# Recurrent layer of a four-layer network: gate products on unsplit float32 operands, GpSimd's multiplications moved to VectorE, a tile of its own for the recurrence's result, longer lags

## The chip, the cores and the metric

One core of a Trainium2 chip runs the whole network in one launch. The metric is the device time of that core in microseconds. Before the change it was 1740.22 us, the median of three runs (1738.8 to 1741.41).

## The reference

Four layers work on 256 tokens of width 1024 (the first two on a second stream of 256 tokens too). The third layer's first half is the recurrent mixer, and it alone is changed:

```python
def rg_lru(x, w_a, b_a, w_x, b_x, lam):
    xb = x.reshape(bsz, s, N_LRU_BLOCKS, LRU_BLOCK)
    r = jax.nn.sigmoid(jnp.einsum("bsnd,nde->bsne", xb, w_a).reshape(bsz, s, w) + b_a)
    i = jax.nn.sigmoid(jnp.einsum("bsnd,nde->bsne", xb, w_x).reshape(bsz, s, w) + b_x)
    log_a = (-LRU_C * r.astype(jnp.float32)) * jax.nn.softplus(-lam.astype(jnp.float32))
    a = jnp.exp(log_a)
    mult = jnp.sqrt(-jnp.expm1(2.0 * log_a))
    u = mult * (i * x).astype(jnp.float32)
    ...  # h[t] = a[t] * h[t-1] + u[t]

def recurrent_mixer(...):
    gate, xr = jnp.split(hn @ w_in, 2, axis=-1)
    xr = causal_depthwise_conv(xr, conv_w, conv_b)
    y = rg_lru(xr, gate_a_w, gate_a_b, gate_x_w, gate_x_b, lam)
    return (y * jax.nn.gelu(gate)) @ w_out
```

The width of the recurrence is 1408, which is 11 tiles of 128 channels. The two gate products are block-diagonal with 16 blocks of 88 channels, so a tile of gates needs two or three tiles of xr: 31 pairs of tiles in all, and 62 products of 128 x 128 weights with 128 x 256 activations.

## The kernel before

Activations stand with channels on partitions and the 256 tokens along the free axis. Every large product is made in three matmuls of a reduced-precision float32 type (fp32r): weights and activations are each split into a rounded high part and a rest, and `mm3` (L338 to L340) adds high x high, high x low and low x high into one PSUM bank. `load_w` (L309 to L315) fetches a weight piece into the buffer `st`, rounds it on ScalarE (`wh`, L311) and subtracts on VectorE (`wl`, L315). There are 6 buffers of `st` and 6 of the pair `wh`, `wl`.

`lru_layer` (L1336) runs over tiles m. Per tile:

- `up(m)` makes tile m of xr: 24 matmuls into a bank called `up`; `leave` (L506, L508) takes it out of PSUM on VectorE into `ldu`, `full` (L512) adds a bias on ScalarE, and `sink_x` applies the convolution, one instruction on ScalarE (L1347) and three on VectorE (L1350), into `xv`. It then splits `xv` into `xh` (ScalarE, L1351) and `xl` (GpSimd, L1352), which the gate products read.
- `gates(m)` loads the gate weights, makes 12 or 18 matmuls into the bank `gt` (L1374), and works out a, the input's factor and the recurrence: tanh, tanh, exp, tanh on ScalarE (L1379 to L1382), then on VectorE the start value and two Newton steps of an inverse square root (L1384 to L1389, a square on ScalarE in each, L1387). GpSimd multiplies twice (L1391, L1393), and a scan on VectorE (L1394) writes the result over `xv`. The eight intermediate rows stand in two buffers `w1`, `w2` of a ring of 4 (tag `lw`), so two tiles of gates fit.
- `sink_g(g)` takes a tile of the other half of the input projection (again 24 matmuls into a bank `up`), applies gelu on ScalarE and VectorE (L1356 to L1359), multiplies by the recurrence's result on GpSimd (L1360) and splits into `yh`, `yl` (L1362, L1363).
- `acc.step(k)` adds the product of y tile k and its output weights to four banks `da` (24 matmuls).

The program before the loop makes xr tiles 0 to 5. In iteration m the order is `up(m + 6)`, `gates(m)`, `sink_g(m - 2)`, `acc.step(m - 5)`; the constants are `LRU_UP` and `LRU_LAGS`. TensorE keeps this written order. On the other engines a scheduler sets the order within their queues when the program is built. Four PSUM banks are shared by `up` and `gt`; the other four are `da`.

Of the kernel before, what the change touches and what calls it, by code (L numbers as in the profile page):

```python
# [10 lines left out]
F32 = mybir.dt.float32  # L11
F32R = mybir.dt.float32r
I32 = mybir.dt.int32
AF = mybir.ActivationFunctionType
ALU = mybir.AluOpType
AX = mybir.AxisListType

P = 128
KD = 8
T = 256  # L20
# [43 lines left out]
NEWTON = [(-1.407904506, 1.681913909), (-1.0, 1.50000036)]  # L64
# [38 lines left out]
EV = ("SSV", "SV", "SVVS")  # L103
TAIL_PRIO = 300
ACC_BUFS = 3
LRU_LAGS = (2, 5, 2)
LRU_UP = 6
PS_FF = (4, 0)
LRU_BUFS = (9, 8, 6)
LAG_FFN = (4, 2)  # L110
LAG_MLP = (6, 2)
RSTD_AT = (4, 7)
# [61 lines left out]
def tile_kernel(ctx: ExitStack, tc: tile.TileContext, I, out, taps=None):  # L174
    nc = tc.nc
    V, S, G, TE = nc.vector, nc.scalar, nc.gpsimd, nc.tensor
# [17 lines left out]
    wbufs = [0, 0]  # L194
    prio = [PRIO0]
# [10 lines left out]
    def tl(name, shape, dt=F32, tag=None, bufs=1, pool="g"):  # L206
        return pools[pool].tile([P] + list(shape), dt, name=name, tag=tag or name, bufs=bufs)

    def lt(name, shape, dt=F32):
        return tl(name, shape, dt, "l", 6)  # L210
# [7 lines left out]
    def bank(name, shape=(512,)):  # L218
        return pools["ps"].tile([P] + list(shape), F32, name=name, tag="b", bufs=psum["b"])
# [17 lines left out]
    def f(ap):  # L237
        return ap.bitcast(F32)
# [12 lines left out]
    def col(name, i=0, n=None):  # L251
        o, w = COLS[name]
        return cols[:, o + i:o + (w if n is None else i + n)]
# [52 lines left out]
    def load_w(src, n=1024, raw=False):  # L306
        with tc.high_priority(offset=prio[0]):
            st = tl("st", [1024], F32, "st", wbufs[0], "w")
            nc.sync.dma_start(st[:, :n], src)  # L309
            hi, lo = [tl("w" + x, [1024], F32R, "w" + x, wbufs[1], "w") for x in "hl"]  # L310
            S.copy(hi[:, :n], st[:, :n])  # L311
            eng = G if pool_next.pop(0) == "G" else V
            if not pool_next:
                pool_next.append("V")
            eng.tensor_tensor(lo[:, :n], st[:, :n], f(hi[:, :n]), ALU.subtract)  # L315
        return (hi, lo, st) if raw else (hi, lo)
# [20 lines left out]
    def mm3(ps, wh, wl, ah, al, first, last, **kw):  # L337
        TE.matmul(ps, lhsT=wh, rhs=ah, start=first, stop=False, **kw)  # L338
        TE.matmul(ps, lhsT=wh, rhs=al, start=False, stop=False, **kw)  # L339
        TE.matmul(ps, lhsT=wl, rhs=ah, start=False, stop=last, **kw)  # L340
# [970 lines left out]
    def lru_softplus():  # L1311


        lam = col("lam")
        n = LRU_K
        t = [st_(f"sp{j}", [n]) for j in range(6)]
        V.tensor_scalar(t[0], lam, -1.0, None, ALU.mult)
        V.tensor_tensor(t[0], t[0], lam, ALU.min)
        S.activation(t[1], t[0], AF.Exp)
        V.tensor_scalar(t[2], t[1], 2.0, None, ALU.add)  # L1320
        V.reciprocal(t[2], t[2])
        V.tensor_tensor(t[2], t[2], t[1], ALU.mult)
        V.tensor_tensor(t[3], t[2], t[2], ALU.mult)
        V.memset(t[4], 1.0 / 17.0)
        for d in (15.0, 13.0, 11.0, 9.0, 7.0, 5.0, 3.0, 1.0):
            V.tensor_tensor(t[4], t[4], t[3], ALU.mult)
            V.tensor_scalar(t[4], t[4], 1.0 / d, None, ALU.add)
        V.scalar_tensor_tensor(t[4], t[4], 2.0, t[2], ALU.mult, ALU.mult)
        V.tensor_scalar(t[5], lam, -1.0, 0.0, ALU.mult, ALU.max)
        V.tensor_tensor(t[4], t[4], t[5], ALU.add)  # L1330
        sp4 = tl("sp4", [2, n])
        V.tensor_scalar(sp4[:, 0, :], t[4], -4.0, None, ALU.mult)
        V.tensor_scalar(sp4[:, 1, :], t[4], 4.0, None, ALU.mult)
        return sp4

    def lru_layer(x, ahead, mod, nxt):  # L1336
        sp4 = lru_softplus()
        hgb = tl("hgb", [22])
        o = COLS["lga"][0]
        V.tensor_scalar(hgb, cols[:, o:o + 22], 0.5, None, ALU.mult)  # L1340
        xs, ys = {}, {}
        lcw = col("lcw")

        def sink_x(m, ps):
            c, (xh, xl) = xs[m] = (tl("xv", [T], F32, "xv", LRU_BUFS[0], "f"),
                                   [tl("x" + y, [T], F32R, "x" + y, LRU_BUFS[1], "f") for y in "hl"])
            S.activation(c, ps, AF.Identity, scale=lcw[:, 33 + m:34 + m], bias=col("lcb", m, 1))  # L1347
            for d in range(1, 4):
                w = lcw[:, (3 - d) * 11 + m:(3 - d) * 11 + m + 1]
                V.scalar_tensor_tensor(c[:, d:], ps[:, :T - d], w, c[:, d:], ALU.mult, ALU.add)  # L1350
            S.copy(xh, c)  # L1351
            G.tensor_tensor(xl, c, f(xh), ALU.subtract)  # L1352

        def sink_g(m, ps):
            sq = lt("lsq", [T])
            S.activation(sq, ps, AF.Square)  # L1356
            V.scalar_tensor_tensor(sq, sq, GELU_IN, ps, ALU.add, ALU.mult)
            S.activation(sq, sq, AF.Tanh, scale=GELU_SC)
            V.scalar_tensor_tensor(sq, sq, 1.0, ps, ALU.add, ALU.mult)  # L1359
            G.tensor_tensor(sq, sq, xs[m][0], ALU.mult)  # L1360
            yh, yl = ys[m] = [tl("y" + y, [T], F32R, "y" + y, LRU_BUFS[2], "f") for y in "hl"]
            S.activation(yh, sq, AF.Copy, scale=0.5)  # L1362
            V.scalar_tensor_tensor(yl, sq, 0.5, f(yh), ALU.mult, ALU.subtract)  # L1363

        def gates(m):
            ks = [k for (mm, k) in GATE_PAIRS if mm == m]
            j0 = [j for j, (mm, k) in enumerate(GATE_PAIRS) if mm == m][0]
            n = len(ks)
            wh, wl = load_w(I["gates"][:, j0:j0 + n].rearrange("p j x c -> p (j x c)"), n * 2 * P)
            b2 = bank("gt", [2, T])  # L1370
            for y in range(2):
                for j, k in enumerate(ks):
                    w = slice((2 * j + y) * P, (2 * j + y + 1) * P)
                    mm3(b2[:, y], wh[:, w], wl[:, w], *xs[k][1], j == 0, j == n - 1)  # L1374
            w1 = tl("w1", [4, T], F32, "lw", 4, "f")
            tr, ti, tau, pv_ = (w1[:, j, :] for j in range(4))
            w2 = tl("w2", [4, T], F32, "lw", 4, "f")
            y, b, u, a = (w2[:, j, :] for j in range(4))
            S.activation(tr, b2[:, 0], AF.Tanh, scale=0.5, bias=hgb[:, m:m + 1])  # L1379
            S.activation(ti, b2[:, 1], AF.Tanh, scale=0.5, bias=hgb[:, 11 + m:12 + m])  # L1380
            S.activation(a, tr, AF.Exp, scale=sp4[:, 0, m:m + 1], bias=sp4[:, 0, m:m + 1])
            S.activation(tau, tr, AF.Tanh, scale=sp4[:, 1, m:m + 1], bias=sp4[:, 1, m:m + 1])  # L1382

            V.scalar_tensor_tensor(pv_, tau, 1.0, tau, ALU.add, ALU.mult)  # L1384
            V.tensor_scalar(y.bitcast(I32), pv_.bitcast(I32), -0.5, RSQRT_SEED, ALU.mult, ALU.add)
            for (c1, c0) in NEWTON:
                S.activation(b, y, AF.Square)  # L1387
                V.scalar_tensor_tensor(b, b, c1, pv_, ALU.mult, ALU.mult)
                V.scalar_tensor_tensor(y, b, c0, y, ALU.add, ALU.mult)  # L1389
            xm = xs[m][0]  # L1390
            G.tensor_tensor(y, y, tau, ALU.mult)  # L1391
            V.scalar_tensor_tensor(u, ti, 1.0, xm, ALU.add, ALU.mult)
            G.tensor_tensor(u, u, y, ALU.mult)  # L1393
            V.tensor_tensor_scan(xm, a, u, 0.0, ALU.mult, ALU.add)  # L1394

        def up(m):
            sink_x(m, ahead.full(ahead.out(load_w(I["lru_in"][1, m]))))

        ws = [load_w(I["lru_in"][1, j]) for j in range(4)]
        with tc.high_priority(offset=LEAD_PRIO):  # L1400
            for j, u in enumerate(ahead.lead(ws)):
                sink_x(j, ahead.full(u))
        for m in range(4, LRU_UP):
            up(m)
        acc = DownAcc(LRU_K, LRU_LAGS[2])
        sink = resid_sink(x, mod[:, 16:24], nxt)
        for m in range(LRU_K + LRU_LAGS[1]):
            k = m - LRU_LAGS[1]
            if m + LRU_UP < LRU_K:
                up(m + LRU_UP)  # L1410
            if m < LRU_K:
                gates(m)
            if 0 <= m - LRU_LAGS[0] < LRU_K:
                g = m - LRU_LAGS[0]
                sink_g(g, ahead.full(ahead.out(load_w(I["lru_in"][0, g]))))
            if k >= 0:
                acc.step(k, I["lru_out"][k], ys[k], sink)
        tap("xl", x)
# [185 lines left out]
    hs = [hl(f"h0{s}", "d") for s in range(2)]  # L1604
# [132 lines left out]
    hs = []  # L1737
# [44 lines left out]
    x, mod = res[0], mods[0]  # L1782
# [193 lines left out]
```

## Time and profile before

| | |
|---|---|
| median of three runs | 1740.22 us |
| the profiled execution | 1737.93 us |
| its span, first to last instruction | 1736.2 us |
| TensorE busy | 1625.7 us (94%) |
| VectorE busy | 1367.9 us (79%) |
| ScalarE busy | 916.7 us (53%) |
| GpSimd busy | 139.8 us (8%) |

In the profile PE is TensorE's matmul, PEld its weight load, DVE VectorE, ACT ScalarE, POOL GpSimd and SP the queue that issues the loads. Times within the span are microseconds from its start. The recurrent layer stands from about 1056 to 1214 us. A busy share over the whole span says little of one layer, so the rows below are cut to the layer's stretch.

### The profile page before, as it was taken

What the parts mean: (1) busy time and instruction counts of PE and PEld (TensorE: products, weight loads), DVE (VectorE), ACT (ScalarE), POOL (GpSimd) and SP (SyncE); (2) the same over time, 40 slices, a digit from 0 to 9 for tenths busy, and PEclk for the clock granted to TensorE, in tenths of its full rate; (3) what the DMA queues carried; (4) which work ended last, traced back from release to release, by engine and by line L of the source; (5) the groups of instructions that cost most, each with busy time, mean ns of one, the idle gap of its engine ahead of it and who ended that gap; (6) DMA issues with size and microseconds to landing.
All of it is one profiled execution on the core that took longest, in us unless ns stands there. A gap on an engine that the chain in (4) does not pass through costs nothing.

```text
span 1736.2 us, 28828 instructions
## 1 busy us (share of the span) xinstructions
PE 1625.7 (94%) x10858; PEld 1404.7 (81%) x10858; DVE 1367.9 (79%) x2799; ACT 916.7 (53%) x1617; POOL 139.8 (8%) x199
## 2 busy tenths in 40 slices
PE   6998989899999998888999999886999999899999
PEld 3784559788888887764899999886999977499999
DVE  5768757589999967778689887987989988569554
ACT  3437654343242434546577666775655554656553
POOL 1110220000000000101000001532000001300000
PEclk9999999999999999999999999998999999999999
DMA  8306536335768633236655553445889843578552
GB/s 309 135 25 225 175 119 205 115 121 186 271 222 303 234 106 104 85 109 207 216 185 183 183 186 127 131 149 183 284 316 345 340 152 128 207 255 288 186 184 72
DMA packets 90714, 327.91 MB, mean 189 GB/s; under 512 B 10064, under 2 KB 10192, under 8 KB 90064
## 3 DMA queue, kind: packets, MB, share of 16 engines
q1 hardware_dynamic: 90288, 323.99, 54.6%
q0 software_dynamic: 288, 2.10, 0.3%
q8 instruction: 85, 1.39, 0.3%
q14 instruction: 53, 0.43, 0.1%
HBM read 325.00 MB, written 1.05 MB: 188 GB/s over the span
## 4 chain that ended last, share of the span: by engine, by line
PE 58%; issue 15%; DVE 9%; POOL 2%; DMA 2%; ACT 2%; POOLq 0%; DVEq 0%; ACTq 0%
PE up L338 8%; PE up L339 8%; PE up L340 7%; PE da L339 4%; PE da L338 4%; PE da L340 4%; DVE wl L315 3%; PE dn L338 2%; PE dn L340 2%; PE dn L339 2%; PE dt L603 2%; PE dt L601 2%; PE dt L602 2%; DMA gst<-in_ada_dram 2%; PE gv L353 1%
## 5 line engine op out<-in xcount | busy, mean ns | idle before, releaser
L311 ACT CAST wh<-st 128x1024 fp32r<-128x1024 f32 (+3 forms) x392 | 400.5, 1030 | 363.6 <-PE up L339 145.2
L315 DVE TENSOR_TENSOR wl<-st,wh 128x1024 fp32r<-128x1024 f32 (+3 forms) x392 | 470.8, 1205 | 95.8 <-ACT wh L311 94.9
L338 PE MATMUL up<-xgh,wh 128*128 128x258 f32 x912 | 259.9, 285 | 5.7 <-DVE ldu L508 3.3
L339 PE MATMUL up<-xgl,wh 128*128 128x258 f32 x912 | 259.8, 285 | 0.0
L340 PE MATMUL up<-xgh,wl 128*128 128x258 f32 x912 | 258.7, 284 | 1.0 <-DVE wl L315 0.9
L338 PEld LDWEIGHTS up<-xgh,wh 128*128 128x128 f32 x912 | 173.4, 190 | 6.6 <-issue 2.2
L340 PEld LDWEIGHTS up<-xgh,wl 128*128 128x128 f32 x912 | 174.6, 191 | 1.4 <-DVE wl L315 1.4
L339 PEld LDWEIGHTS up<-xgl,wh 128*128 128x128 f32 x912 | 174.0, 191 | 0.0
L386 DVE CUSTOM_DVE_ANT_0 gst<-gst,crow,cols 128x1024 f32<-128x1024 f32 x120 | 153.4, 1283 | 14.3 <-DMA gst<-in_kvada_dram 6.7
L338 PE MATMUL up<-h2h,wh 128*128 128x512 f32 (+1 forms) x384 | 143.8, 375 | 5.3 <-ACT h2h L448 5.1
L340 PE MATMUL up<-h2h,wl 128*128 128x512 f32 (+1 forms) x384 | 143.5, 374 | 0.5 <-DVE wl L315 0.5
L338 PE MATMUL da<-g2h,wh 128*128 128x256 f32 x512 | 143.9, 281 | 0.0
L340 PE MATMUL da<-g2h,wl 128*128 128x256 f32 x512 | 143.8, 281 | 0.0
L339 PE MATMUL da<-g2l,wh 128*128 128x256 f32 x512 | 143.7, 281 | 0.0
L339 PE MATMUL up<-h2l,wh 128*128 128x512 f32 (+1 forms) x384 | 143.3, 373 | 0.3 <-DVE h2l L449 0.3
L339 PEld LDWEIGHTS da<-g2l,wh 128*128 128x128 f32 x512 | 96.5, 188 | 0.0
L340 PEld LDWEIGHTS da<-g2h,wl 128*128 128x128 f32 x512 | 96.4, 188 | 0.0
L338 PEld LDWEIGHTS da<-g2h,wh 128*128 128x128 f32 x512 | 96.4, 188 | 0.0
L353 PE MATMUL gv<-gst,cst 128*32 128x512 f32 x352 | 68.7, 658 | 22.5 <-DMA gst<-in_w_ada_dram 15.5
L338 PEld LDWEIGHTS up<-h2h,wh 128*128 128x128 f32 x384 | 73.1, 190 | 18.5 <-ACT h2h L448 5.5
L340 PEld LDWEIGHTS up<-h2h,wl 128*128 128x128 f32 x384 | 73.0, 190 | 13.6 <-DVE wl L315 1.0
L339 PEld LDWEIGHTS up<-h2l,wh 128*128 128x128 f32 x384 | 73.1, 190 | 12.9 <-DVE h2l L449 0.5
(498 smaller groups left out, 3920.8 us busy)
## 6 DMA issues: line engine op xcount, KB each, us to landing
st<-in_mlp_dram SPq DMA_DIRECT2D x128, 512.0 KB, 4.6
gst<-in_w_ada_dram SPq DMA_DIRECT2D x96, 512.0 KB, 4.4
st<-in_w_up_dram SPq DMA_DIRECT2D x88, 512.0 KB, 4.3
gst<-in_ada_dram SPq DMA_DIRECT2D x40, 512.0 KB, 4.2
st<-in_w_in_dram SPq DMA_DIRECT2D x32, 512.0 KB, 3.6
gst<-in_ada21t_dram SPq DMA_DIRECT2D x32, 512.0 KB, 6.4
st<-in_w_down_dram SPq DMA_DIRECT2D x25, 512.0 KB, 3.8
gst<-in_ada20t_dram SPq DMA_DIRECT2D x24, 512.0 KB, 4.6
```

The source lines that it names most:

```text
L311: S.copy(hi[:, :n], st[:, :n])
L315: eng.tensor_tensor(lo[:, :n], st[:, :n], f(hi[:, :n]), ALU.subtract)
L338: TE.matmul(ps, lhsT=wh, rhs=ah, start=first, stop=False, **kw)
L339: TE.matmul(ps, lhsT=wh, rhs=al, start=False, stop=False, **kw)
L340: TE.matmul(ps, lhsT=wl, rhs=ah, start=False, stop=last, **kw)
L353: TE.matmul(ps[32 * t:32 * t + 32, :], lhsT=cst[:, 2 * q + i, :], rhs=st[:, i * 512:i * 512 + 512], start=(q < 2), stop=(q >= 2), tile_pos ...
L386: V.tensor_tensor_reduce(o, st, r, 0.5, bias[:, b:b + 1], ALU.mult, ALU.add, dest[:, v, b:b + 1])
L601: TE.matmul(o, lhsT=hh[:, k, js], rhs=wh[:, wsl], start=(k == 0), stop=False)
L602: TE.matmul(o, lhsT=hh[:, k, js], rhs=wl[:, wsl], start=False, stop=False)
L603: TE.matmul(o, lhsT=hlo[:, k, js], rhs=wh[:, wsl], start=False, stop=(k == KD - 1))
```

## The change

`gates` no longer splits its operands: it loads the weights into `st` and makes one plain float32 matmul per pair from `st` and `xv`. `xh` and `xl` go. The three multiplications of GpSimd go to VectorE, where the factor's second Newton step is applied to the product itself instead of to the root. The scan writes a tile `hv` of its own. The lags become 3 for `sink_g` and 6 for `acc.step`.

```diff
-LRU_LAGS = (2, 5, 2)
+LRU_LAGS = (3, 6, 2)
-LRU_BUFS = (9, 8, 6)
+LRU_BUFS = (9, 5, 6)
...
         def sink_x(m, ps):
-            c, (xh, xl) = xs[m] = (tl("xv", [T], F32, "xv", LRU_BUFS[0], "f"),
-                                   [tl("x" + y, [T], F32R, "x" + y, LRU_BUFS[1], "f") for y in "hl"])
+            c = xs[m] = tl("xv", [T], F32, "xv", LRU_BUFS[0], "f")
...
-            S.copy(xh, c)
-            G.tensor_tensor(xl, c, f(xh), ALU.subtract)
...
             S.activation(sq, sq, AF.Tanh, scale=GELU_SC)
+            V.tensor_tensor(ps, ps, hs.pop(m), ALU.mult)
             V.scalar_tensor_tensor(sq, sq, 1.0, ps, ALU.add, ALU.mult)
-            G.tensor_tensor(sq, sq, xs[m][0], ALU.mult)
...
-            wh, wl = load_w(I["gates"][:, j0:j0 + n].rearrange("p j x c -> p (j x c)"), n * 2 * P)
+            with tc.high_priority(offset=prio[0]):
+                st = tl("st", [1024], F32, "st", wbufs[0], "w")
+                nc.sync.dma_start(st[:, :n * 2 * P], I["gates"][:, j0:j0 + n].rearrange("p j x c -> p (j x c)"))
...
-                    w = slice((2 * j + y) * P, (2 * j + y + 1) * P)
-                    mm3(b2[:, y], wh[:, w], wl[:, w], *xs[k][1], j == 0, j == n - 1)
+                    TE.matmul(b2[:, y], lhsT=st[:, (2 * j + y) * P:(2 * j + y + 1) * P], rhs=xs[k], start=(j == 0),
+                              stop=(j == n - 1))
...
-            for (c1, c0) in NEWTON:
-                S.activation(b, y, AF.Square)
-                V.scalar_tensor_tensor(b, b, c1, pv_, ALU.mult, ALU.mult)
-                V.scalar_tensor_tensor(y, b, c0, y, ALU.add, ALU.mult)
-            xm = xs[m][0]
-            G.tensor_tensor(y, y, tau, ALU.mult)
-            V.scalar_tensor_tensor(u, ti, 1.0, xm, ALU.add, ALU.mult)
-            G.tensor_tensor(u, u, y, ALU.mult)
-            V.tensor_tensor_scan(xm, a, u, 0.0, ALU.mult, ALU.add)
+            (c1, c0), (d1, d0) = NEWTON
+            S.activation(b, y, AF.Square)
+            V.scalar_tensor_tensor(b, b, c1, pv_, ALU.mult, ALU.mult)
+            V.scalar_tensor_tensor(y, b, c0, y, ALU.add, ALU.mult)
+
+            V.scalar_tensor_tensor(u, ti, 1.0, xs[m], ALU.add, ALU.mult)
+            V.tensor_tensor(u, u, tau, ALU.mult)
+            S.activation(b, y, AF.Square)
+            V.tensor_tensor(u, u, y, ALU.mult)
+            V.scalar_tensor_tensor(b, b, d1, pv_, ALU.mult, ALU.mult)
+            V.scalar_tensor_tensor(u, b, d0, u, ALU.add, ALU.mult)
+            h = hs[m] = tl("hv", [T], F32, "hv", LRU_BUFS[1], "f")
+            V.tensor_tensor_scan(h, a, u, 0.0, ALU.mult, ALU.add)
```

The scheduler also reorders the queues. On GpSimd, the stretch of the loop from the third tile on, the change against before (`w_` with a number is a tile's `w1` or `w2`, `lsq` is gelu's):

```order
-L1352 TENSOR_TENSOR xl<-xv,xh 128x256
-L1391 TENSOR_TENSOR w_11540<-w_11540,w_11539 128x256
-L1393 TENSOR_TENSOR w_11540<-w_11540 128x256
-L1360 TENSOR_TENSOR lsq<-lsq,xv 128x256
-L1352 TENSOR_TENSOR xl<-xv,xh 128x256
-L1391 TENSOR_TENSOR w_11674<-w_11674,w_11673 128x256
-L1393 TENSOR_TENSOR w_11674<-w_11674 128x256
-L1360 TENSOR_TENSOR lsq<-lsq,xv 128x256
```

Nothing takes their place: GpSimd has no instruction left in the layer.

On VectorE before, the end of the fourth tile of gates (`w_11674`) and what stands around it, the split of the next gate weights (768 columns) among it:

```order
L315 TENSOR_TENSOR wl<-st,wh 128x1024
L1388 SCALAR_TENSOR_TENSOR w_11674<-w_11674,w_11673 128x256
L506 COPY ldc<-up 128x1
L508 TENSOR_TENSOR ldu<-up,rb 128x256
L1389 SCALAR_TENSOR_TENSOR w_11674<-w_11674 128x256
L1357 SCALAR_TENSOR_TENSOR lsq<-lsq,ldu 128x256
L315 TENSOR_TENSOR wl<-st,wh 128x768
L1394 SCALAR_TENSOR_TENSOR xv<-w_11674 128x256
L1359 SCALAR_TENSOR_TENSOR lsq<-lsq,ldu 128x256
```

The row that writes `xv` is the scan, and between L1389 and it GpSimd's two multiplications run.

On VectorE now, the same part of a tile's work two tiles later (`w_11720`, line numbers of the changed kernel; `hv` is written by the scan):

```order
L1388 SCALAR_TENSOR_TENSOR w_11720<-w_11720,w_11719 128x256
L1392 TENSOR_TENSOR w_11720<-w_11720,w_11719 128x256
L1389 SCALAR_TENSOR_TENSOR w_11720<-w_11720 128x256
L506 COPY ldc<-up 128x1
L508 TENSOR_TENSOR ldu<-up,rb 128x256
L1394 TENSOR_TENSOR w_11720<-w_11720 128x256
L1395 SCALAR_TENSOR_TENSOR w_11720<-w_11720,w_11719 128x256
L1384 SCALAR_TENSOR_TENSOR w_11793<-w_11793 128x256
L1396 SCALAR_TENSOR_TENSOR w_11720<-w_11720 128x256
L1354 SCALAR_TENSOR_TENSOR lsq<-lsq,ldu 128x256
L1398 SCALAR_TENSOR_TENSOR hv<-w_11720 128x256
L1356 TENSOR_TENSOR ldu<-ldu,hv 128x256
```

The multiplications L1392, L1394 and L1356 are new on this engine, no split of gate weights is left, and the scan follows its own engine's row L1396.

## Rows read from the trace of the kernel before

**Rows 1.** Busy time by engine over the whole span (share, instructions)

```profile
PE 1625.7 (94%) x10858; PEld 1404.7 (81%) x10858; DVE 1367.9 (79%) x2799; ACT 916.7 (53%) x1617; POOL 139.8 (8%) x199
```

**Rows 2.** Stretches: us, busy of PE, PEld, DVE, ACT, POOL; clock, DMA share, GB/s

```profile
1069.00:1206.00 137.00, 111.44 (x840) 106.75 (x838) 116.65 (x237) 95.47 (x186) 53.82 (x44) 0.94 0.49 154
1069.00:1121.00 52.00, 43.83 (x349) 42.11 (x348) 46.77 (x98) 41.90 (x83) 26.13 (x17) 1.00 0.44 131
1121.00:1150.00 29.00, 26.21 (x186) 26.01 (x185) 24.81 (x53) 20.45 (x42) 10.63 (x10) 0.83 0.46 142
1150.00:1180.00 30.00, 27.68 (x224) 26.64 (x224) 25.64 (x51) 21.55 (x41) 9.80 (x9) 1.00 0.51 162
1180.00:1206.00 26.00, 13.72 (x88) 11.99 (x86) 19.43 (x38) 11.58 (x23) 7.25 (x8) 0.87 0.61 204
```

**Rows 3.** PE's waits, 1069 to 1206: who for whom; us in total, times, longest

```profile
PE da L338 <- ACT yh L1362: 9.2, 4, 5.7
PE gt L340 <- DVE wl L315: 3.4, 2, 2.8
PE up L338 <- DVE ldu L508: 3.3, 3, 2.0
PE gt L339 <- POOL xl L1352: 2.0, 2, 1.0
PE da L339 <- DVE yl L1363: 2.0, 3, 0.9
PE da L340 <- DVE wl L315: 1.6, 2, 1.1
PE gt L338 <- ACT w L1380: 1.6, 2, 1.2
```

**Rows 4.** Groups on POOL, 1069 to 1206: busy, mean ns, idle before

```profile
L1352 POOL TENSOR_TENSOR xl<-xv,xh 128x256 fp32r<-128x256 f32 x11 | 23.5, 2148 | 256.2 <-ACT xh L1351 256.2
L1391 POOL TENSOR_TENSOR w<-w,w 128x256 f32<-128x256 f32 x11 | 13.4, 1215 | 36.0 <-DVE w L1389 20.1 <-ACT lsq L1358 15.9
```

**Rows 5.** Groups on DVE, 1069 to 1206, same columns

```profile
L315 DVE TENSOR_TENSOR wl<-st,wh 128x768 fp32r<-128x768 f32 x9 | 9.6, 1066 | 0.0
L1394 DVE TENSOR_TENSOR_SCAN xv<-w 128x256 f32<-128x256 f32 x11 | 9.2, 832 | 14.2 <-POOL w L1393 14.2
L1392 DVE SCALAR_TENSOR_TENSOR w<-w,xv 128x256 f32<-128x256 f32 x11 | 6.7, 610 | 0.0
L315 DVE TENSOR_TENSOR wl<-st,wh 128x512 fp32r<-128x512 f32 x2 | 1.4, 680 | 0.0
```

**Rows 6.** PE in order of time, recurrent layer's start: us of start, us, what

```profile
1069.12 0.29 PE L339 MATMUL up<-xgl,wh 128*128 128x258 f32 x1
1069.24 0.29 PE L340 MATMUL up<-xgh,wl 128*128 128x258 f32 x1
```

**Rows 7.** PE in order of time, attention: float32 products with 64 columns

```profile
209.81 1.95 PE L708 MATMUL opb<-pt,Vt 128*64 128x256 f32 x16
211.69 0.66 PE L689 MATMUL tr<-kc,zqb 128*128 128x128 f32 x4
```

**Rows 8.** Single matmuls' durations by tile: ns least/median/most

```profile
L708 PE MATMUL opb<-pt,Vt x160: 379/379/687, 209.8 to 839.0; 128*64 128x256 f32 x160
L339 PE MATMUL gt<-xl,wh x62: 276/281/415, 1078.9 to 1167.6; 128*128 128x256 f32 x62
```

**Rows 9.** PE in order of time, keys' projection: products of 512 columns

```profile
1470.42 0.40 PE L601 MATMUL dt<-wh,kvh 128*128 128x512 f32 x1
1470.66 0.39 PE L602 MATMUL dt<-wl,kvh 128*128 128x512 f32 x1
```

**Rows 10.** DVE in order of time, between two of POOL's instructions

```profile
1142.46 0.41 DVE L1357 SCALAR_TENSOR_TENSOR lsq<-lsq,ldu 128x256 f32<-128x256 f32 x1
1142.79 0.41 DVE L1389 SCALAR_TENSOR_TENSOR w<-w 128x256 f32<-128x256 f32 x1
```

**Rows 11.** Chain that ended last, one tile's first tanh and its scan

```profile
1081.81 0.47 ACT w L1379
1098.64 0.69 DVE xv L1394
```

**Rows 12.** DMA issues: KB each, median us to landing

```profile
st<-in_lru_in_dram SPq DMA_DIRECT2D x22, 512.0 KB, 4.3
```

**Rows 13.** Row sums of a float32 matrix, PE in order of time

```profile
1061.67 1.40 PE L416 MATMUL nps<-ones,acc 128*128 128x2 f32 x12
1062.92 0.36 PE L338 MATMUL da<-xgh,wh 128*128 128x258 f32 x1
```

More of the change, by code (lines that the diff above doesn't have):

```diff
@@ L1340, in lru_layer @@
         V.tensor_scalar(hgb, cols[:, o:o + 22], 0.5, None, ALU.mult)
-        xs, ys = {}, {}
+        xs, hs, ys = {}, {}, {}
         lcw = col("lcw")
         def sink_x(m, ps):
-            c, (xh, xl) = xs[m] = (tl("xv", [T], F32, "xv", LRU_BUFS[0], "f"),
-                                   [tl("x" + y, [T], F32R, "x" + y, LRU_BUFS[1], "f") for y in "hl"])
+            c = xs[m] = tl("xv", [T], F32, "xv", LRU_BUFS[0], "f")
             S.activation(c, ps, AF.Identity, scale=lcw[:, 33 + m:34 + m], bias=col("lcb", m, 1))
```

## The prediction

> **What bounds the kernel now.** I read first the busy time by engine, then the recurrent layer's stretch cut into pieces, then TensorE's waits in it, then the groups on GpSimd and VectorE that stand behind them. Over the whole span TensorE is 94% busy [rows 1], so little is to be had elsewhere. From 1069 us (the layer's lead-in of four tiles is done) to 1206 us (its last output products), TensorE is busy in 111.4 of 137.0 us, and its granted clock averages 0.94 [rows 2]. So 25.6 us are idle, and part of the rest runs at half speed.
>
> The pieces of the stretch [rows 2] differ. From 1069 to 1121 TensorE idles 8.2 us, from 1121 to 1180 5.1 us, from 1180 to 1206 12.3 us. The clock is 0.83 from 1121 to 1150 and 0.87 in the last piece. Between levels of 1.2 and 2.4 GHz, a mean of 0.83 says that 34% of 29 us, 9.9 us, ran at the lower level, which lost half of that, 4.9 us; likewise 26% of the last 26 us lost 3.4 us. Both pieces come behind or hold waits of TensorE.
>
> TensorE's waits [rows 3] name four causes. It waits for `xl`, GpSimd's rest of xr (2.0 us); for gate weights that VectorE splits late (3.4); for banks that ScalarE's tanh or VectorE's `ldu` has not emptied (1.6 and 3.3); and, most of all, for `yh` and `yl` at the end (9.2 and 2.0), with 1.6 for output weights. Behind these stands GpSimd: 11 rests of 2148 ns on the mean, and a first multiplication of 1215 ns [rows 4]. VectorE, busy 116.65 of 137 us [rows 2], idles 14.2 us before its 11 scans, until GpSimd's second multiplication is done [rows 5]. It is an in-order queue, so each such idle delays the weight splits and bank readings behind it.
>
> **The change part by part.**
>
> *Gate products.* 186 fp32r matmuls go. Two in a row start 0.12 us apart [rows 6], so they fill 22.3 us. 62 float32 matmuls come. The trace writes two records for each such matmul: for the row sums the program has 6 (three partial sums, two token halves), the trace 12 [rows 13]. So 124 records are to be priced, and no row has one with 128 x 128 weights and 256 columns. The nearest is attention's, with 64 columns of weights: it lasts 379 ns, against 281 ns for an fp32r one [rows 8]. An fp32r matmul of 512 columns lasts 0.40 us and is followed after 0.24 us [rows 9]. I take 0.24, since the record lasts about as long: 124 x 0.24 = 29.8 us, that is **+7.5 us**. Below, attention's 16 records take 1.88 us [rows 7], 0.1175 each: 14.6 us, or -7.7 us; but their weights fill half the array, and two may run side by side. Above, a weight load that nothing hides adds what a record of two columns takes, 1.25 us / 12 = 0.104 us [rows 13]: 124 x 0.344 = 42.7 us, or +20.4 us. The Trainium skill (FP8 and Floating Point Precision, TensorE Precision Notes) says that true FP32 takes four passes through the array, which speaks against the change: four passes in place of three would be an estimated 29.8 us and +7.5, where attention's row taken as it stands would give -7.7; no run here shows a full-width one.
>
> *GpSimd.* All 53.8 us of its work in the stretch [rows 2] go. This counts only through who waited: the 2.0 us for `xl`, the 1.6 us of banks held by a tanh that could not start before GpSimd had read its buffers, and VectorE's 14.2 us.
>
> *VectorE.* 11 splits of gate weights go, 9.6 + 1.4 = 11.0 us busy [rows 5]. Three instructions per tile come, 33 in all. Undisturbed, such instructions start 0.33 us apart [rows 10]: 10.9 us. So its work stays level, but two disturbances leave: the scans' waits, and the slowing beside GpSimd (L1392 takes 610 ns on the mean, the scan 832 [rows 5], where undisturbed ones take about 410 [rows 10] and 690 [rows 11]; 11 x 0.34 = 3.7 us for these two alone). VectorE's 116.65 us become about 111, in a stretch that I expect to last 116: it stays almost as full as TensorE, so I don't let all waits go.
>
> *ScalarE.* It loses the rounding of gate weights and `xh`, 22 instructions. At 95.5 of 137 us [rows 2] it isn't the bound; I count nothing. Were it the bound, its tanh would hold the banks, as in the rivals.
>
> *Loads.* The gate weights now stay in one of the six buffers `st` until their products have run; the load that reuses it waits so long on the SP queue, and those behind it too. A load lands after 4.3 us [rows 12], and the split takes some 2 us more. Six loads stand for two iterations or more, at least 2 x 5.8 us of TensorE's work (24 x 0.12 + 12 x 0.24). That hides it: 0 us; uncovered it would cost up to 6 us at a tile.
>
> *Lags.* The last gates get two more weight blocks (`sink_g` of a tile and one `acc.step`, 24 x 0.12 = 2.9 us each) of TensorE's work between them and the products that need them, 5.8 us. This covers the longest wait of the end, 5.7 us [rows 3]. No work is added.
>
> *The sum.* From 1069 to 1121 I let 6.5 of 8.2 us go (`xl`, tanh, most of the late `ldu`). From 1121 to 1180 4.1 of 5.1 (the gate weights' 3.4 and part of what is late behind them), with 4.4 of the 4.9 us of slow clock. From 1180 on 10.3 of 12.3, with 3.0 of 3.4. Together -28.3 us; with +7.5, **-20.8 us**. What stays late next is VectorE's queue, with weight splits and `ldu` in the iterations that hold all parts. The profiled execution took 1737.93 us (a span of 1736.2 and 1.7 around it) and lies 2.3 us below the median of 1740.22. So 1737.93 - 20.8 = 1717.1, and for a median **1719 us**.
>
> **The rivals.**
>
> *A, only the named causes go.* VectorE's queue paces the layer as before, with hops to ScalarE where those to GpSimd were. Then `xl` 2.0, gate weights 3.4, tanh 1.6 and half of the slow clock (4.2) go: -11.2 + 7.5 = -3.7, about 1736 us. For it speaks VectorE's 85% share; against it, that its own waits name GpSimd [rows 5].
>
> *B, dear products.* Every weight load is exposed: -28.3 + 20.4 = -7.9, 1732 us. Against it: loads run beside matmuls (PEld and PE are both busy over 100 of 137 us [rows 2]).
>
> *C, nothing stays late.* All 25.6 us and 8.3 us of slow clock go: -33.9 + 7.5 = -26.4, 1714 us; with the low price of the products -41.6, 1699 us. Against it: VectorE's 111 us of work hardly fit below 112 us.
>
> *D, slower.* VectorE gets no relief: its queue has 22 instructions more (33 come, 11 go), its idle 20.35 us stays because each tile's factor still goes to ScalarE for two squares, and each instruction that comes takes 0.41 us: 116.65 - 11.0 + 13.5 + 20.35 = 139.5, +2.5 us, and the products' +7.5 fall where TensorE has no slack: +10 us, 1750 us. It decides the time once VectorE's work and waits exceed 137 us. Against it: 14.2 of the 20.35 us end with GpSimd. The Trainium skill (VectorE: DVE Perf Modes, Rules for kernel authors) says to keep the count of chained VectorE instructions low, and the change raises it; by that rule alone this rival would be the forecast, and no run yet shows it.
>
> **How the numbers follow.** The forecast (a gain of 12 to 28 us) gets 0.67, A 0.12, B 0.07, C 0.08, D 0.06. The range from 1709 to 1732 holds the forecast, B and most of C; it leaves out D, A and C's low end, about 0.2. A measurement of this kernel tells some 0.2%, 3.5 us, from no change. Faster by more: 0.67 + 0.07 + 0.08 and 0.07 of A, 0.89. Within: the rest of A, 0.05. Slower: D, 0.06.
>
> **What would show it.** Right: records of `gt` about 380 ns long, 124 of them, some 0.24 us apart; no GpSimd work in the layer; the scan following VectorE's own rows without idle time; TensorE idle under 8 us in the stretch; the clock near 1.00 throughout; the wait for `yh` under 2 us. Wrong: `gt` records further than 0.3 us apart (B); TensorE idle as before with waits for `ldu` and ScalarE's tanh (A, D); waits for `st` loads. A difference outside the layer would contradict me too.

## The result, and the profile after

The changed kernel takes 1709.87 us (median of four runs, 1708.99 to 1712.81); the kernel before took 1740.63 us in the four runs beside it. The ratio is 0.9824, 95% interval 0.9811 to 0.9838: faster by 1.8%, inside the range and at its low end, 9 us below the forecast of 1719. The profiled execution took 1710.57 us with a span of 1708.8 us, against 1737.93 and 1736.2. One run of the kernel before, beside number 12 below, took 8177.62 us and is left out of the ratio there.

Busy time by engine over the whole span, first line of the page (before: [rows 1]):

```profile
PE 1617.7 (95%) x10796; PEld 1398.4 (82%) x10796; DVE 1360.1 (80%) x2821; ACT 905.1 (53%) x1595; POOL 86.5 (5%) x155
```

TensorE lost 62 instructions: 186 matmuls went and 124 records came. VectorE gained 22, as counted. To compare the layer as a whole I cut both traces from the first product of its lead-in to the first product of the next layer's (columns as in [rows 2]). The kernel before:

```profile
1055.80:1212.99 157.19, 131.55 (x993) 126.69 (x993) 129.81 (x273) 103.62 (x205) 53.82 (x44) 0.93 0.47 150
```

The kernel after, the layer, and then the same pieces as in [rows 2]:

```profile
1055.46:1185.93 130.47, 124.68 (x930) 120.09 (x931) 122.86 (x296) 92.61 (x184) 0.00 (x0) 1.00 0.52 168
...
1069.00:1121.00 52.00, 52.00 (x370) 49.87 (x369) 51.15 (x126) 39.94 (x80) 0.00 (x0) 1.00 0.52 161
1121.00:1150.00 29.00, 29.00 (x212) 27.91 (x211) 28.61 (x70) 22.56 (x44) 0.00 (x0) 1.00 0.56 180
1150.00:1180.00 30.00, 25.21 (x201) 24.01 (x201) 28.61 (x63) 20.76 (x40) 0.00 (x0) 1.00 0.65 215
1180.00:1206.00 26.00, 23.96 (x199) 23.61 (x198) 24.43 (x52) 15.61 (x30) 0.00 (x0) 1.00 0.78 257
```

The layer went from 157.2 to 130.5 us. That is 26.7 of the 27.4 us by which the spans differ, so the gain is the layer's. In the first two pieces TensorE has no idle time at all, the clock is 1.00 everywhere, and the last piece belongs for the most part to the next layer (from 1185.93). The third column of busy times says what comes next: VectorE is busy in 122.9 of the 130.5 us, nearly as full as TensorE (124.7).

TensorE's waits in the layer, same columns as [rows 3]; of the causes there, `xl`, the tanh, `ldu` and the late weight splits are gone:

```profile
PE da L338 <- ACT yh L1359: 3.8, 2, 2.0
PE da L338 <- DVE xres L526: 1.0, 1, 1.0
PE da L339 <- DVE yl L1360: 0.9, 2, 0.6
```

The gate products by tile (ns least/median/most), and in order of time one tile's and what follows it:

```profile
L1373 PE MATMUL gt<-xv,st x124: 377/379/379, 1077.3 to 1146.9; 128*128 128x256 f32 x124
```

```profile
1081.93 2.75 PE L1373 MATMUL gt<-xv,st 128*128 128x256 f32 x12
1084.34 0.47 PE L338 MATMUL up<-xgh,wh 128*128 128x258 f32 x1
```

Twelve records take 1084.34 - 1081.93 = 2.41 us, 0.20 each, although each lasts 379 ns: the next starts when half of it is over. All 124 fill about 24.9 us.

VectorE's groups in the layer (columns as in [rows 5]): the scan has no idle time before it and takes 680 ns where it took 832:

```profile
L315 DVE TENSOR_TENSOR wl<-st,wh 128x1024 fp32r<-128x1024 f32 x33 | 39.9, 1214 | 0.3 <-ACT wh L311 0.3
L1398 DVE TENSOR_TENSOR_SCAN hv<-w 128x256 f32<-128x256 f32 x11 | 7.5, 680 | 0.0
```

Where TensorE still idles: in order of time, its last waits of the layer (idle time before in brackets).

```profile
1169.76 0.27 PE L340 MATMUL da<-yh,wl 128*128 128x256 f32 x1
1172.00 0.39 PE L338 MATMUL da<-yh,wh 128*128 128x256 f32 x1 [1.96 <-ACT yh L1359]
...
1179.00 0.38 PE L338 MATMUL da<-yh,wh 128*128 128x256 f32 x1 [1.80 <-ACT yh L1359]
```

And VectorE in the same time, gelu's steps (`lsq`, `ldu`) towards that `yh`:

```profile
1166.55 2.34 DVE L315 TENSOR_TENSOR wl<-st,wh 128x1024 fp32r<-128x1024 f32 x2
1168.82 0.41 DVE L1354 SCALAR_TENSOR_TENSOR lsq<-lsq,ldu 128x256 f32<-128x256 f32 x1
1169.15 1.21 DVE L315 TENSOR_TENSOR wl<-st,wh 128x1024 fp32r<-128x1024 f32 x1
1170.29 0.41 DVE L1356 TENSOR_TENSOR ldu<-ldu,hv 128x256 f32<-128x256 f32 x1
1170.62 0.14 DVE L506 COPY ldc<-up 128x1 f32<-128x1 f32 x1
1170.69 0.41 DVE L508 TENSOR_TENSOR ldu<-up,rb 128x256 f32<-128x256 f32 x1
1171.02 0.41 DVE L1357 SCALAR_TENSOR_TENSOR lsq<-lsq,ldu 128x256 f32<-128x256 f32 x1
```

Each starts before the one ahead has wholly ended, none waits for another engine, and weight splits stand between the steps: so I read the tile as late because VectorE's queue is full. The row names ScalarE (`yh`), but ScalarE only had to wait for L1357.

### The profile page after: what moved, and what is told of

It is laid out like the page before. It is cut to its first block, busy times and chain, and to the rows that moved or that the text cites. A ratio compares the mean times of both kernels' runs of the same rounds, so it can differ in the third digit from the quotient of the medians.

```text
span 1708.8 us, 28624 instructions
## 1 busy us (share of the span) xinstructions
PE 1617.7 (95%) x10796; PEld 1398.4 (82%) x10796; DVE 1360.1 (80%) x2821; ACT 905.1 (53%) x1595; POOL 86.5 (5%) x155
## 4 chain that ended last, share of the span: by engine, by line
PE 72%; DVE 9%; DMA 3%; ACT 2%; issue 2%; POOL 0%; SPq 0%; DVEq 0%; ACTq 0%; POOLq 0%
PE up L338 10%; PE up L339 10%; PE up L340 10%; PE da L338 6%; PE da L339 6%; PE da L340 6%; DVE wl L315 2%; PE dn L338 2%; PE dn L340 2%; PE dn L339 2%; PE dt L601 2%; PE dt L603 2%; PE dt L602 2%; DMA gst<-in_ada_dram 2%; PE gv L353 1%
## 5 line engine op out<-in xcount | busy, mean ns | idle before, releaser
L311 ACT CAST wh<-st 128x1024 fp32r<-128x1024 f32 (+2 forms) x381 | 392.2, 1037 | 359.3 <-PE up L339 137.2
L315 DVE TENSOR_TENSOR wl<-st,wh 128x1024 fp32r<-128x1024 f32 (+2 forms) x381 | 458.4, 1207 | 93.4 <-ACT wh L311 92.0
```

## The experiments

All ratios are to the kernel before, in the same batch, with 95% intervals. The executions begin the layer up to some 7 us earlier or later (1050 to 1057 us here, behind parts that are the same in all), and what follows it takes 523 to 529 us, so I compare its length too, cut as above, one execution of each kernel. TensorE's idle time in the layer is its length less TensorE's busy time; the same work takes more busy time where the clock is lower.

| kernel | ratio | layer, us | TensorE busy | VectorE busy | clock |
|---|---|---|---|---|---|
| before | 1 | 157.2 | 131.6 | 129.8 | 0.93 |
| after | 0.9824 | 130.5 | 124.7 | 122.9 | 1.00 |
| 1 products alone | 0.9917 | 143.2 | 131.5 | 118.5 | 0.94 |
| 2 multiplications alone | 0.9947 | 147.0 | 126.1 | 134.1 | 0.97 |
| 3 lags alone | 0.9989 | 158.2 | 130.6 | 130.8 | 0.96 |
| 4 after, old lags | 0.9848 | 130.7 | 125.9 | 122.9 | 0.99 |
| 5 after, 11 more multiplications | 0.9872 | 135.8 | 129.2 | 127.0 | 0.96 |
| 6 after, half the gate products | 0.985 | 137.3 | 120.6 | 123.4 | 0.94 |
| 7 after, gelu first at the end | 0.9835 | 132.1 | 126.3 | 122.9 | 0.99 |
| 8 after, float32 output, tiles 7 to 10 | 0.9862 | 133.4 | 128.2 | 120.7 | 0.97 |
| 9 after, float32 output, tiles 0 to 5 | 0.9829 | 129.9 | 127.6 | 116.2 | 1.00 |
| 10 after, float32 output, tiles 0 to 2 | 0.9839 | 128.8 | 125.6 | 119.8 | 1.00 |
| 11 after, float32 output, all tiles | 0.9838 | 129.7 | 129.7 | 109.3 | 1.00 |
| 12 numbers 11 and 6 together | 0.9784 | 122.5 | 117.8 | 107.8 | 1.00 |

### 1 to 4: which part gives the gain

Three theories share the change out: the gain comes from the products (P), from the multiplications that leave GpSimd, so that VectorE's queue no longer waits (V), or from the lags at the layer's end (L).

**1. Products alone.** Before, with the products of the change and the scan's own tile; GpSimd multiplies as before, lags 2 and 5.

```diff
-            S.copy(xh, c)
-            G.tensor_tensor(xl, c, f(xh), ALU.subtract)
...
-                    mm3(b2[:, y], wh[:, w], wl[:, w], *xs[k][1], j == 0, j == n - 1)
+                    TE.matmul(b2[:, y], lhsT=st[:, (2 * j + y) * P:(2 * j + y + 1) * P], rhs=xs[k], start=(j == 0),
+                              stop=(j == n - 1))
...
-            V.tensor_tensor_scan(xm, a, u, 0.0, ALU.mult, ALU.add)
+            V.tensor_tensor_scan(h, a, u, 0.0, ALU.mult, ALU.add)
```

> The kernel before with the unsplit gate products and the result's own tile alone; GpSimd keeps its three multiplications per tile, the lags stay 2 and 5. Theory V (VectorE's queue sets the layer's pace, and its idle time before the scans, until GpSimd has multiplied, is the main loss): those 14 us of idle time stay for the most part, 11 us of weight splits leave VectorE; about 12 us faster than before (1728). Theory P (what was late were the split operands of the gate products): most of the change's 27 to 31 us, 20 us or more (1720 or less). Theory L (the lags): under 8 us.

Measured: 1723.36 us, 0.9917 (0.9896 to 0.9938), some 14 us: between what V and P foresaw, and nearer V. The layer is 14.0 us shorter. VectorE's busy time falls by 11.3 us, the splits; its waits for GpSimd stay (waits of VectorE, 1069 to 1206 us):

```profile
DVE hv L1395 <- POOL w L1393: 13.5, 9, 2.1
```

TensorE's idle time falls by 14.0 us. Its granted clock is still 0.94, and it waits 4.6 us for `yh` and 4.7 for `yl`.

**2. Multiplications alone.** Before, with GpSimd's three multiplications on VectorE and the second Newton step on the product; products split, scan in place, lags 2 and 5.

```diff
-            G.tensor_tensor(y, y, tau, ALU.mult)
...
-            G.tensor_tensor(u, u, y, ALU.mult)
...
+            V.tensor_tensor(u, u, tau, ALU.mult)
+            S.activation(b, y, AF.Square)
+            V.tensor_tensor(u, u, y, ALU.mult)
...
```

> The kernel before with the three multiplications per tile moved from GpSimd to VectorE (and the second Newton step applied to the product) alone; gate products split as before, with GpSimd making xl, old lags. Theory V: the scans' 14 us of idle time go, 11 us of work come to a queue that also keeps the 11 us of splits: about 8 us faster (1732), and VectorE without idle time. Theory P: within 4 us of before. Theory L: the same.

Measured: 1728.6 us, 0.9947 (0.9928 to 0.9966), which V foresaw and P did not; the layer is 10.2 us shorter. VectorE has more work than any other run (134.1 us), and from 1150 to 1180 us no gap at all; TensorE still waits 7.3 us for `yh` (before 9.2, [rows 3]). Its idle time falls by 4.7 us, and its busy time by 5.5 with the same work, which is the clock. Window and waits of this kernel:

```profile
1150.00:1180.00 30.00, 28.70 (x236) 28.25 (x237) 30.00 (x70) 22.66 (x42) 0.00 (x0) 1.00 0.62 189
```

```profile
PE da L338 <- ACT yh L1362: 7.3, 3, 3.5
PE up L338 <- DVE ldu L508: 4.2, 3, 2.0
PE up L340 <- DVE wl L315: 3.9, 3, 1.9
```

**3 and 4. Lags.** Before with lags 3 and 6 (and a tenth `xv`, since the scan still writes there), and the changed kernel with 2 and 5.

```diff
-LRU_LAGS = (2, 5, 2)
+LRU_LAGS = (3, 6, 2)
```

> The kernel before with the lags 3 and 6 alone (and 10 buffers of xv, which the longer lag needs). Theory L: 10 us or more faster (1730 or less), since the 9 to 13 us that TensorE waits for yh and yl at the layer's end go. Theories V and P: VectorE's queue is as late as before, so 5 us at most (1735 or more).

> The changed kernel with the old lags 2 and 5. Theory L: it loses 10 us or more against the changed kernel (1720 or more). Theories V and P: VectorE is still full, so what the lags cover at the end is a few us; 2 to 6 us are lost (1712 to 1716).

Measured: 1735.8 us, 0.9989 (0.9976 to 1.0002), and 1710.99 us, 0.9848 (0.9824 to 0.9872), with layers of 158.2 and 130.7 us. The lags are worth nothing that can be measured, in either kernel; L falls, and so do the 2 to 6 us that V and P foresaw as lost in number 4. In number 3 the wait for `yh` does shrink, from 9.2 to 6.9 us, but the waits for `yl` (2.0 to 4.6) and tanh (2.5 to 4.3) grow by more.

The two parts that count give 14.0 + 10.2 = 24.2 us apart and 26.7 together. What they share is VectorE's queue: its busy time and its wait for GpSimd before the scan are 129.8 + 14.2 = 144.0 us before, 132.0 in number 1, 134.1 in number 2, 122.9 after, which is 12.0, 9.9 and 21.1 us less where the layer is 14.0, 10.2 and 26.7 us shorter. That this queue is the cause fits these sums, and number 5 tests it; number 1 takes away the splits of the gate products' operands and VectorE's work on them at once, and does not part the two.

### 5 to 7: what paces the layer now

Theory Q: VectorE's queue still does.

**5. Eleven more multiplications**, one per tile of gates, by ones.

```diff
             V.tensor_tensor(u, u, tau, ALU.mult)
+            V.tensor_tensor(u, u, wz, ALU.mult)
```

> The changed kernel with one multiplication by one more per tile on VectorE, in the chain before the scan: 11 x 0.335 = 3.7 us more work there. Theory Q (after the change VectorE's queue, full from 1069 to 1179 us, sets the layer's pace and TensorE only looks busy beside it): 3.5 us or more lost, about 1714. Theory T (TensorE's own products, back to back until 1170 us, set the pace and VectorE is just in time): 1 us or less.

Measured: 1717.41 us, 0.9872 (0.9855 to 0.9889). Some 3.7 us of VectorE work cost 5.3 us of layer. Little of that is idle time of TensorE, which grows by only 0.8 us (5.8 to 6.6): the wait for `yh` is 3.1 us (3.8 in the changed kernel), and `yl` (2.0 for 0.9) and `wl` (1.4 for none) are later. The other 4.5 us are TensorE's busy time with the same work, 129.2 for 124.7: the clock is lower behind the waits (0.69 in the layer's last 11 us). The layer, and two pieces of it:

```profile
1055.26:1191.07 135.81, 129.23 (x930) 124.14 (x931) 126.97 (x308) 92.50 (x185) 0.00 (x0) 0.96 0.50 161
...
1121.00:1150.00 29.00, 29.00 (x213) 27.93 (x212) 29.00 (x72) 21.36 (x44) 0.00 (x0) 1.00 0.50 169
1150.00:1180.00 30.00, 25.55 (x192) 24.34 (x190) 29.64 (x65) 19.82 (x37) 0.00 (x0) 0.94 0.69 217
```

So VectorE has nothing to spare at the layer's end, and most of the price of more work there comes through the clock.

**6. Half of the gate products.** 31 of 62.

```diff
-            for y in range(2):
+            for y in range(1):
...
-            S.activation(ti, b2[:, 1], AF.Tanh
+            S.activation(ti, b2[:, 0], AF.Tanh
```

> The changed kernel with the second of the two gate products of each pair left out (the input gate is then worked out from the first product): 31 float32 products, 62 records of 0.20 us, 12.5 us less for TensorE, and nothing less for VectorE. Theory T: 10 us or more faster than the changed kernel (1700 or less). Theory Q: 3 us at most, and the time comes back as waits of TensorE for ldu, wl or yh.

Measured: 1713.54 us, 0.985 (0.9829 to 0.9872): 12.5 us of TensorE's work gone, and the layer is 6.9 us *longer*. The work came back as waits and as a lower clock (the layer and two pieces, then waits of TensorE in the layer):

```profile
1050.54:1187.87 137.33, 120.63 (x869) 115.15 (x870) 123.40 (x296) 92.15 (x184) 0.00 (x0) 0.94 0.50 160
...
1121.00:1150.00 29.00, 25.82 (x184) 25.22 (x183) 27.15 (x64) 22.35 (x45) 0.00 (x0) 0.88 0.54 173
1150.00:1180.00 30.00, 21.15 (x143) 19.07 (x142) 26.48 (x55) 15.90 (x31) 0.00 (x0) 0.91 0.62 202
```

```profile
PE da L338 <- ACT yh L1359: 5.1, 3, 2.4
PE up L340 <- DVE wl L315: 3.1, 2, 2.9
PE da L340 <- DVE wl L315: 3.0, 3, 1.4
PE da L339 <- DVE yl L1360: 2.6, 3, 1.0
```

TensorE's idle time grows from 5.8 to 16.7 us, by 10.9, so most of the work left out became waits. Its busy time falls by 4.1 us and not by 12.5; the other 8.4 are the lower clock. Together: -12.5 + 10.9 + 8.4 = 6.8 us. Without the loss of clock the layer would be some 1.6 us shorter (an estimate from these numbers; no run holds the clock up). Theory T, 10 us faster, falls; Q foresaw the waits, but no longer layer.

**7. Gelu first at the end.** Tiles 8 to 10 of `sink_g` go ahead in the queues.

```diff
-                sink_g(g, ahead.full(ahead.out(load_w(I["lru_in"][0, g]))))
+                with tc.high_priority(offset=TAIL_PRIO if g >= 8 else 0):
+                    sink_g(g, ahead.full(ahead.out(load_w(I["lru_in"][0, g]))))
```

> The changed kernel with the work behind the last three products of the second half of the input projection raised in the scheduler's priority, so that it stands ahead of the next layer's weight splits on VectorE. If TensorE's 5 us of waits at the layer's end for yh and yl come from the order of VectorE's queue alone, they go: 3 to 5 us faster than the changed kernel (1706). If VectorE is simply out of time (theory Q), the splits that are moved back make the next layer's start late by as much: within 1 us.

Measured: 1710.12 us, 0.9835 (0.9813 to 0.9856), no gain, as Q foresaw. The wait moved: 0.8 us for `yh` are left, and in their place stand (waits of TensorE)

```profile
PE gt L1373 <- ACT w L1380: 2.3, 1, 2.3
PE da L339 <- DVE yl L1360: 1.1, 2, 0.9
```

Another order of the full queue only chose who is late.

### 8 to 12: relief for VectorE

The output products on unsplit operands take a weight split (1.2 us) and a `yl` (0.33) per tile off VectorE and cost TensorE, by the price found above, 8 x (0.40 - 0.36) = 0.3 us. Which tiles is one condition (numbers 9 and 10 ask `m < Y_F32`):

```diff
+            if m >= Y_F32:
+                ys[m] = tl("yf", [T], F32, "yf", LRU_BUFS[2], "f")
+                S.activation(ys[m], sq, AF.Copy, scale=0.5)
+                return
...
+            if not isinstance(act, list):
+                TE.matmul(self.ps(m), lhsT=w[:, ms], rhs=act, start=(k == 0 and m < 4), stop=(k == self.nk - 1),
+                          skip_group_check=True)
+                return
```

**8. Tiles 7 to 10**, where TensorE still waits.

> The changed kernel with the output product of the last four tiles made on unsplit float32 operands too. VectorE loses 4 weight splits and 4 splits of y, 4 x 1.14 + 4 x 0.335 = 5.9 us; TensorE gets 32 products of 0.40 us in place of 96 of 0.12: 1.3 us more. Theory Q: 4 us or more faster (1706 or less), the waits for yh and yl go. Theory T: between 1 us slower and 3 us faster.

Measured: 1717.45 us, 0.9862 (0.9841 to 0.9883), slower than the changed kernel, which neither theory foresaw. The five runs lie in two groups, 1710.1 and 1711.8 us, and 1717.5 to 1718.4; the profiled one is the slowest. Of the 7.8 us by which it is above that of the changed kernel, the layer holds 2.9, and 6.1 come behind the layer (1.2 less ahead of it), which I did not follow. In the layer TensorE idles no longer than in the changed kernel (5.2 us for 5.8), but one wait of 4.85 us stands ahead of the last 30 records, and these take 8.8 us where 0.20 each would be 6.0: the clock again (0.97 for the layer). How that wait arises is read from this one trace: the output weights now hold `st` until their products have run, the next layer's loads come late, and ScalarE, which rounds those weights in its order, waits for them, 1.2 us of it just ahead of tile 10's `yf`. Waits of ScalarE from 1150 to 1185 us, then TensorE in order of time:

```profile
ACT wh L312 <- DMA st<-in_mlp_dram: 3.4, 4, 1.2
```

```profile
1166.33 7.61 PE L572 MATMUL da<-yf,st 128*128 128x256 f32 x34 [0.36 <-ACT yf L1370]
1178.78 9.17 PE L572 MATMUL da<-yf,st 128*128 128x256 f32 x30 [4.85 <-ACT yf L1370]
```

**9 to 11. Tiles 0 to 5, tiles 0 to 2, and all tiles.**

> The changed kernel, with the output product of y tiles 0 to 5 on unsplit float32 operands (their weights stay in st, no wh and wl, no yl). Six weight splits of 1.2 us and six rests of y of 0.33 us leave VectorE, 9 us in all; TensorE gets 6 x 8 x (0.40 - 0.36) = 2 us more. Theory Q (VectorE's queue paces the layer): the layer gets 5 to 9 us shorter, ratio to before 0.977 to 0.980, and VectorE has slack in the loop. Rival (the buffers st pace, held by float32 weights until their products have run, as with tiles 7 to 10): no faster than the changed kernel, 0.982 to 0.986, with waits of TensorE or ScalarE for loads.

> The same for y tiles 0 to 2 alone: 4.6 us leave VectorE, 1 us comes to TensorE. Theory Q: about half the gain of the run with six tiles, ratio 0.979 to 0.981. Rival (buffers st pace): 0.982 to 0.984.

> The same for all 11 y tiles: 17 us leave VectorE, 3.5 us come to TensorE. If the loss of the run with tiles 7 to 10 came from late loads behind them, it stays (+4 to +7 us) and adds to what the early tiles give: ratio 0.979 to 0.985. If that loss came from something that only a mix of both kinds makes, this run is the fastest: below 0.977.

Measured: 1710.86 us, 0.9829 (0.981 to 0.9847); 1710.96 us, 0.9839 (0.9825 to 0.9853); 1712.21 us, 0.9838 (0.9816 to 0.9859). None is faster than the changed kernel, although VectorE's busy time in the layer fell from 122.9 to 116.2, 119.8 and 109.3 us. The numbers are those of the rival, but not for its reason: no wait of TensorE for a load or for a held buffer stands in these layers. ScalarE does wait for loads (7.6 us in number 11, 4.4 in the changed kernel), but in number 11 TensorE has no idle time that this could make. The layer with all tiles shows what holds it:

```profile
1050.31:1180.05 129.74, 129.74 (x843) 121.69 (x843) 109.28 (x273) 84.23 (x174) 0.00 (x0) 1.00 0.50 164
```

TensorE is busy in 129.74 of 129.74 us. It is now the bound alone. Its busy time grew by 5.1 us, more than the 11 x 0.3 = 3.5 reckoned (between other products, 16 records take 3.27 to 3.45 us here, for 2.88 of the 24 fp32r matmuls: 0.4 to 0.6 us per tile), and that is what the removed waits, 5.8 us, gave. So theory Q alone is too simple: relief of VectorE that TensorE pays for gives nothing either. Relief of VectorE without dearer products was not run; as TensorE idles 5.8 us in the changed kernel at full clock, it could give about that at most (an estimate).

**12. Both.** All output products unsplit, and half of the gate products left out.

> All output products on unsplit float32 operands (17 us off VectorE, 3.5 us more on TensorE) and 31 of the 62 gate products left out (12.5 us off TensorE; the input gate's own product is left out, and its tanh reads the recurrence gate's). Each of the two alone made the layer no shorter. Theory B2 (in the changed kernel TensorE and VectorE are about equally full, so that relief of one alone gives nothing): together they do, the layer falls from 130.5 to 117 to 124 us, ratio 0.972 to 0.979. Rival (a third resource, the loads or ScalarE's queue, paces at about 130 us): no gain, layer 129 to 137 us, ratio 0.982 to 0.987.

Measured: 1703.43 us, 0.9784 (0.9764 to 0.9803):

```profile
1055.43:1177.92 122.49, 117.79 (x780) 109.97 (x781) 107.75 (x273) 83.65 (x174) 0.00 (x0) 1.00 0.54 174
```

The layer is 8.0 us shorter than the changed kernel's, as theory B2 foresaw, where relief of VectorE paid for by TensorE gave 0.7 us (number 11) and relief of TensorE alone cost 6.9 (number 6, 8.4 of it clock). So neither a third engine nor the loads hold the layer at 130 us, and less work for TensorE shortens it only once VectorE is relieved too. Two engines about equally full fit all of this. No version that computes everything beat the changed kernel measurably.

## Why the prediction was right, and where it was off

- **Product price: mis-sized.** The step "I take 0.24, since the record lasts about as long" failed. The records are 379 ns long, as read from attention's row, and 124 in number, but 0.20 us apart (the twelve records above): 24.9 us instead of 29.8, so +2.6 us instead of +7.5. This is 4.9 of the miss. A record's length did not tell its spacing. The low bound of 0.1175 [rows 7], half-filled weights, was no guide for full ones either. The four passes that the Trainium skill (FP8 and Floating Point Precision, TensorE Precision Notes) gives true FP32 would make an estimated 0.48 us per product at the 0.12 us of [rows 6]; measured are 2 x 0.20 = 0.40, and the measurement decides.
- **Waits: right in sum.** Forecast: 6.5 + 4.1 + 10.3 = 20.9 us of idle time go. In the layer it fell from 157.19 - 131.55 = 25.6 to 130.47 - 124.68 = 5.8 us, by 19.9. The places were not all right: I left 1 to 2 us in each piece, and the trace has none before 1169.8 us and 4.8 us in the piece from 1150 to 1180. Of the signs that I named, two did not come: the spacing of 0.24 us, and a wait for `yh` under 2 us (it is 3.8).
- **Clock: somewhat short.** Forecast 7.4 us. TensorE's busy time fell by 6.9 us while its work grew by 2.6, so the clock gave 9.5. My pieces ended at 1206 us, but the layer ran to 1212.99, and in these last 7 us the clock was 0.76: 48% at the lower level, 1.7 us lost that the sum did not hold.
- **Sum:** 19.9 + 9.5 - 2.6 = 26.7 us instead of 20.8. The other 3.2 of the 9.1 us between forecast and median: 1.9 by which I had raised the forecast above the sum, 0.6 outside the layer, and 0.7 by which the profiled execution of after lies above its median.
- **VectorE: right, and the heart of it.** The two disturbances left as read: scan without idle time, 680 ns for 832. "It stays almost as full as TensorE" holds: 122.9 us of busy time, and in number 5 another 3.7 us of work there cost 5.3 us of layer.
- **Lags: wrong as a cover.** "This covers the longest wait of the end" put 5.8 us of work against a wait of 5.7. Numbers 3 and 4 show that the lags give nothing: in number 3 `yh` is less late by 2.3 us, but `yl` and the tanh are later. That the queue falls as far behind as it is let is my reading and was not tried. So the 10.3 us of the layer's end came from the other two parts, and that this term of the sum held although it leaned on the lags was luck.
- **Loads, ScalarE: 0, right.** No wait of TensorE for a load in the layer, though ScalarE's waits for loads grew from 1.2 to 4.4 us. Number 8 suggests that this cover ends where float32 weights stand just ahead of the next layer.
- **Rivals.** A (only the named causes) fell: its 1736 us needed VectorE to pace at the old length. B fell with the spacing of 0.20. C, nothing stays late, came nearest in time; what stays late is 5.8 us, and the products were cheaper than its main case took. D fell: the rule that the Trainium skill (VectorE: DVE Perf Modes, Rules for kernel authors) gives, to keep the count of chained instructions low, would have cost time here, as 22 more instructions ended waits of 14.2 us; but number 5 bears it out for the kernel as it stands now, where 11 more cost 5.3 us of layer, most of it through the clock.

## What to carry to other kernels

An in-order queue that waits for another engine loses that time for everything behind it: add its waits to its busy time before you call it idle, and price a move by what this sum does (here 144.0 to 122.9 us, for a layer 26.7 us shorter). Here more lag and another order only chose who was late, and work had to go. With two engines both over 94% busy, relief of one showed next to nothing or less than nothing here, so try both together before ruling either out. And split a change of time into TensorE's work, its idle time and its clock: in numbers 5 and 6 the clock was the greater part of what was lost or the whole of it.

## What the runs showed of the hardware that was not expected

- A plain float32 product of 128 x 128 weights and 256 columns appears as two records of 379 ns, 0.20 us apart: 0.40 us, 1.1 times the 0.36 us of three fp32r matmuls that start 0.12 us apart [rows 6], while it saves the splits of both operands.
- Less work can mean a longer time: with 12.5 us less of TensorE's work (number 6) its clock fell to 0.88 and 0.91 in stretches where it is 1.00 with that work, which cost 8.4 us of a layer 6.9 us longer.
- The split of xr on GpSimd, least, median and most of its 11 instructions in the kernel before:

```profile
L1352 POOL TENSOR_TENSOR xl<-xv,xh x11: 730/1642/4357, 1074.5 to 1131.7; 128x256 fp32r<-128x256 f32 x11
```

  The same subtraction takes 0.73 us or six times that. The Trainium skill (SBUF — State Buffer, SBUF: two separate sides) says that a VectorE instruction with two inputs in SBUF and a GpSimd instruction that reads SBUF exclude each other on a shared port for a whole instruction; the trace agrees so far as the spread goes, and VectorE's scan took 832 ns on the mean with GpSimd at work and 680 without. That the port is the cause was not tried by itself.
